# A trunk of attention, retention and convolution on one core: a pool for the operands of the matmuls, longer holds of a PSUM bank, key-value products in column halves, and probabilities scaled by their sum ahead of their transposes

## The chip, the cores and the metric

The kernel runs on one core of a Trainium2 chip. The metric is the device time of the program in microseconds (us). A core has five engines with instruction streams of their own: TensorE (PE in the profile) does matmuls and transposes, and its weight loads are listed apart as PEld; VectorE (DVE) and ScalarE (ACT) do elementwise work, GpSimd (POOL) a few powers, and SyncE (SP) issues the DMAs. Data lie in SBUF, 128 partitions wide; TensorE writes into PSUM, which has 8 banks of 2 KB a partition.

## What is computed

One layer of a causal streaming encoder over 2048 tokens of width 1024, all in float32. On the normalised input one projection feeds three mixers: attention over the own chunk of 64 tokens and 8 chunks before it (6 heads of 64), a gated convolution of 31 taps (256 channels), and retention (6 heads of 64). Their outputs are concatenated and projected, and added to the input. A squared-ReLU MLP of width 4096 follows, and then a gated embedding. Cut to what the change touches:

```python
scores = jnp.einsum('bhncd,bhnkd->bhnck', q, kb).astype(jnp.float32) * (d ** -0.5)
scores = scores + bias[None, :, None]
scores = jnp.where(valid[None, None, :, None, :], scores, -1e30)
probs = jax.nn.softmax(scores, axis=-1).astype(v.dtype)
out = jnp.einsum('bhnck,bhnkd->bhncd', probs, vb)
...
kv = jnp.einsum('bhnmd,bhnme->bhnde', k_dec, vc)
def step(state, kv_c):
    return chunk_decay * state + kv_c, state
...
xf * lax.rsqrt(jnp.mean(xf * xf, axis=-1, keepdims=True) + EPS)
```

## The kernel before

**Tiling.** The tokens are worked in 4 blocks of T = 512 (NB = 4), each block in 4 tiles of 128 (NT = 4). The 6 heads of attention and of retention go in 3 pairs of 128 columns. Activations lie transposed, channels on partitions, in 8 tiles of 128 x 512 (KT = 8).

**Products.** A float32 operand is split into a high part in the matmul's format (fp32r) and the rest, also in fp32r. mm3s then issues three matmuls: high by high, high by low, low by high; it is the three-record group that recurs in the trace. All large products stream 512 or 384 columns. `wunit` brings weights in 1 MB units of HALF = 512 columns into the tile w (6 buffers). In block 0 they come as raw float32 and are split on ScalarE and VectorE (L126, L127); the split form is kept in DRAM, and the later blocks load it whole.

**Where the operands lie.** `big(name, slot)` is a tile of 8 x 512 in one of four buffers big0 to big3 (16 KB a partition each). xh and xl, the split normalised input, use big0 and big1, for the mixers and again (from wo_b, L688, on) for the MLP. mh and ml, the split mixer outputs, use big2 and big3; then hid, the MLP's hidden tile, takes big2 and big3 in turn. `late()` puts the gate's input xh and xl in big2 and big3 for blocks 0 to 2; for the last block ffn2 puts it in big0 and big1. In the matmuls xh, xl, hid, mh and ml are moving operands of 512 columns with blocks of w as weights, but for att_proj and ret_proj, where blocks of xh and xl are the weights and w moves. All of this comes from the pool `sp`, opened after the pool of constants. In the built program w starts at byte 23584 of a partition, big0 and big1 at 72736 and 89120, big2 and big3 at 195712 and 212096.

**Order of the work.** The large products are a chain of segments: per block conv_proj, from block 1 on the gate of the block before, then att_proj and ret_proj for three pairs, wo_a and wo_b (output projection), and eight pairs of ffn1 and ffn2. Each yields after every matmul, and `advance()` then asks whether some other work is due and puts it there: `tasks` at fixed places, and three chains: att_mix (0), ret_mix (1), conv_mix (2). A step of a chain is issued, then its `yield d` sets a hold: the chain's next step comes when `clk`, the planner's own estimate of TensorE's time, is d later. Chains 1 and 2 use one PSUM bank "r" in turn; `rfree` holds either back for 2.0 after the other's step. W lists the holds. TensorE keeps the order so written; the other engines' instructions are ordered by a scheduler from priorities that follow program order, and `tc.high_priority(offset=...)` moves a piece forward or, where negative, back.

**The places that the change touches.**
- rms_split (L230 on) makes xh, xl of the MLP's input, and then the squares and their running sum sq for the norm. norm2 takes the sum when ffn1 has begun.
- att_mix, per token tile t: scores into two banks sc (one a head); a custom VectorE instruction adds the bias and finds the negative maximum nm (L501); ScalarE takes Exp and the row sum into rs (L503); five transposes per head (L59, sc<-ident,pt) and a copy pT; then 20 records of values, po<-pT,v, one tile later. Both the wait for the scores, W["st"], and that for the transposes, W["ts"], are holds. Behind the last tile:

```python
        V.reciprocal(rs[:, 8:16], rs[:, 0:8])
        rb = tmp("rb", T).rearrange("p (t n) -> p t n", n=P)
        V.tensor_copy(rb.rearrange("p t (h d) -> p (t h) d", d=HD),
                      rs[:, 8:16].unsqueeze(2).to_broadcast([P, 8, HD]))
        yield W["vo"]
        ...
            PE.transpose(b[:, i * P : i * P + P], rb[:, i], ident)
        rT = tmp("rT", T)
        A.activation(rT, b[:, :T], AF.Copy)
        values(NT - 1, pT, *span)
        yield 0
        ...
        V.tensor_tensor(rT, po, rT, ALU.mult)
```

- ret_mix: rkv (keys by values, four 128x128 products of which only the two diagonal 64x64 blocks are read by the state updates, L613), then transposes rqT and rkT, scores rsc, their masking rat on VectorE (L638), rout, and a group norm.
- conv_mix: transposes cvt, layer norm z (L402), transposes back cvb, and the pointwise product cpw.

Of the kernel before, what the change touches and what calls it, by code (L numbers as in the profile page):

```python
# [12 lines left out]
F32R = mybir.dt.float32r  # L13
# [20 lines left out]
AHEAD = 2500  # L34
LATE = -1000
AT, RT = (2, 4, 6), (3, 5, 7)
WOA = [(j, k) for ks in ((0, 1, 2, 3), (4, 5)) for j in range(2) for k in ks] + [(j, k) for j in range(2, KT) for k in range(6)]
# [3 lines left out]
def trunk(ctx, tc, a, out):  # L41
# [4 lines left out]
    class PE:  # L46
# [10 lines left out]
        def transpose(o, x, i):  # L57
            clk[0] += 240 / 2200.0
            tc.keep_in_program_order(nc.tensor.transpose(o, x, i))  # L59

    cpool = ctx.enter_context(tc.tile_pool(name="const", bufs=1))
    sp = ctx.enter_context(tc.tile_pool(name="sp", bufs=1))
# [10 lines left out]
    def stile(tag, bufs, shape, name=None, dt=F32):  # L73
        return sp.tile(list(shape), dt, tag=tag, name=name or tag, bufs=bufs)
# [4 lines left out]
    def big(name, slot):  # L79
        return stile(f"big{slot}", 1, [P, 8, T], name, F32R)  # L80

# [40 lines left out]
    def wtile():  # L122
        return stile("w", 6, [P, 2, 2, HALF], "w", F32R)

# [105 lines left out]
    def rms_split(j, gidx, x, sq):  # L230
        h = cur["h"][j]
        g = ng[:, gidx, j : j + 1]
        A.activation(x[0][:, j], h, AF.Copy, scale=g)  # L233
        V.scalar_tensor_tensor(x[1][:, j], h, g, f(x[0][:, j]), ALU.mult, ALU.subtract)  # L234
        if j == 0:
            A.activation(sq, h, AF.Square)
        else:
            q = tmp("q", T)
            A.activation(q, h, AF.Square)
            V.tensor_tensor(sq, sq, q, ALU.add)  # L240

# [18 lines left out]
    cur = {}  # L260
    W = dict(qk=5.0, st=4.5, ts=2.0, vo=1.6, r0=3.5, r1=2.4, r2=1.8, r3=11, c1=5.0, c2=4.0, c3=0.6)

# [120 lines left out]
    def conv_mix():  # L383
# [3 lines left out]
        for u in range(2):  # L387
# [13 lines left out]
            for i in range(2):  # L401
                V.tensor_scalar(z[u][:, i * DC : i * DC + DC], b2[:, i], s6[:, 12 + 2 * i : 13 + 2 * i],  # L402
                                s6[:, 18 + i : 19 + i], ALU.subtract, ALU.mult)
            yield W["c1"]
        hl = []
        for c in range(2):
            b = rbank("cvb")
            for t in range(NT):
                PE.transpose(b[:, t * P : t * P + P], z[t // 2][:, (t % 2) * DC + c * P : (t % 2) * DC + c * P + P], ident)
            u = tmp("u", T)  # L410
            A.activation(ys[c], b, AF.Tanh, bias=cvh[:, 1, c : c + 1], scale=cvh[:, 0, c : c + 1])
            A.activation(u, b, AF.Identity, bias=cvh[:, 1, c : c + 1], scale=cvh[:, 0, c : c + 1])
            V.scalar_tensor_tensor(ys[c], ys[c], 1.0, u, ALU.add, ALU.mult)
            yh, yl = cv("yh", F32R), cv("yl", F32R)
            A.activation(yh, ys[c], AF.Copy)
            V.tensor_tensor(yl, ys[c], f(yh), ALU.subtract)
            hl.append((yh, yl))
            yield W["c2"]
        yield W["c3"]
# [41 lines left out]
    def att_mix(p):  # L461
# [21 lines left out]
        def scores(t):  # L483
# [14 lines left out]
            for h, s in enumerate(ss):  # L498
# [4 lines left out]
                A.activation(pt[:, :n], pt[:, :n], AF.Exp, bias=nm[:, 0:1], scale=-1.0,  # L503
                             accum_out=rs[:, 2 * t + h : 2 * t + h + 1])
                out.append((s, pt, c0 // P, n // P))
            return out
# [29 lines left out]
        for t in range(NT):  # L536
# [6 lines left out]
            if t < NT - 1:  # L543
                rdy = both(t + 1)
        V.reciprocal(rs[:, 8:16], rs[:, 0:8])
        rb = tmp("rb", T).rearrange("p (t n) -> p t n", n=P)
        V.tensor_copy(rb.rearrange("p t (h d) -> p (t h) d", d=HD),
                      rs[:, 8:16].unsqueeze(2).to_broadcast([P, 8, HD]))
        yield W["vo"]
        b = sb2("rT")  # L550
        for i in range(NT):
            PE.transpose(b[:, i * P : i * P + P], rb[:, i], ident)
        rT = tmp("rT", T)
        A.activation(rT, b[:, :T], AF.Copy)
        values(NT - 1, pT, *span)
        yield 0
        kvc[p] = k, v
        mh, ml = mix()
        V.tensor_tensor(rT, po, rT, ALU.mult)
        A.activation(mh[:, AT[p]], rT, AF.Copy)  # L560
        V.tensor_tensor(ml[:, AT[p]], rT, f(mh[:, AT[p]]), ALU.subtract)
        yield 0
# [37 lines left out]
    def ret_mix(p):  # L600
# [7 lines left out]
        for t in range(NT):  # L608
            PE.matmul(b[:, t * P : t * P + P], ns[t][:, P : 2 * P], ns[t][:, 256:384], start=True, stop=True)
        states = [now] + stm + [nxt]  # L610
        for t in range(NT):
            for hr in hrs:
                V.scalar_tensor_tensor(states[t + 1][hr, hr], states[t][hr, hr], gstate[hr, p : p + 1],  # L613
                                       b[hr, t * P + hr.start : t * P + hr.stop], ALU.mult, ALU.add)
        yield W["r0"]
        b = rbank("rqT")
# [5 lines left out]
        A.activation(qT, b, AF.Copy)  # L622
        yield W["r1"]
        b = rbank("rkT")
# [3 lines left out]
        A.activation(kT, b, AF.Copy)  # L628
        yield W["r1"]
        at = stile("rat", 1, [P, NT, 2 * P])  # L630
# [222 lines left out]
    chains = [[], [], []]  # L853
    rfree = [0.0]

    def chain(i, gen, start, end):
# [26 lines left out]
    def advance(pos):  # L883
        posn[0] = pos
        for t in list(tasks):
            while t[0] and t[0][0] <= pos:
# [8 lines left out]
        for c in chains:  # L895
            while c and c[0][0] <= pos:
# [5 lines left out]
                try:  # L902
                    d = next(t[3])
                    t[4] = clk[0] + d + 0.01
                    if c is not chains[0]:
                        rfree[0] = clk[0] + 2.0
                except StopIteration:
# [148 lines left out]
```

## Time and profile before

| | before |
|---|---|
| median of 3 runs | 2718.81 us (2717.66 to 2721.08) |
| the profiled execution's own time | 2718.58 us |
| its span | 2716.6 us |
| granted TensorE clock, mean | 0.996 |
| matmul records on TensorE | 13354 |
| DMA | 533.36 MB, 196 GB/s over the span |

The span is the time from the first to the last instruction that the profile shows; 2.0 us lie around it. Busy time is given per engine. A matmul's record shows how long it is in the array, and successive ones overlap: the pace of a stream is read from the distance of their starts. The granted clock is TensorE's share of its full 2.4 GHz.

### The profile page before, as it was taken

Reading aid. Unit: us, or ns where it says so; the run is one execution under the profiler, and the core shown is the slowest. Engines: PE = TensorE matmul, PEld = TensorE weight load, DVE = VectorE, ACT = ScalarE, POOL = GpSimd, SP = SyncE. Lnnn points to the kernel's source line nnn. Section 1 sums busy time; section 2 is a strip of 40 time slices with the busy share of each in tenths; the row PEclk is TensorE's granted clock in tenths of the full one; section 3 lists DMA queues with packets and bytes.
Section 4 is the critical chain, followed back from the end, with each engine's and each line's share of the span. In section 5 each row is a group of like instructions: output and inputs, shape, how many; then the busy total and the mean of one; then the engine's idle time right before and its main releaser. Section 6 shows DMA issues by size and latency. Waiting matters only on the chain.

```text
span 2716.6 us, 33597 instructions
## 1 busy us (share of the span) xinstructions
PE 2680.4 (99%) x13354; PEld 2216.5 (82%) x13354; DVE 1327.8 (49%) x2649; ACT 764.2 (28%) x1576; POOL 97.0 (4%) x98
## 2 busy tenths in 40 slices
PE   8989999999999999999999999999999999999999
PEld 7777788888888888888888888888888888888887
DVE  7966544458655443334755552222384545222233
ACT  4444423343244222123214331101222432110111
POOL 1010000000010000000001000000000100000000
PEclk9999999999999999999999999999999999999999
DMA  8667656467633567677543455555654354555553
GB/s 285 211 213 244 219 177 208 166 198 267 217 121 140 206 216 261 216 255 261 217 168 121 159 203 192 193 186 191 240 194 170 112 199 142 189 191 187 192 201 125
DMA packets 123708, 533.36 MB, mean 196 GB/s; under 512 B 12832, under 2 KB 39712, under 8 KB 77728
## 3 DMA queue, kind: packets, MB, share of 16 engines
q1 hardware_dynamic: 123552, 531.21, 55.7%
q8 instruction: 106, 1.74, 0.3%
q14 instruction: 50, 0.41, 0.0%
HBM read 410.58 MB, written 120.59 MB: 196 GB/s over the span
## 4 chain that ended last, share of the span: by engine, by line
PE 89%; DVE 6%; DMA 2%; POOL 1%; ACT 1%; issue 1%; SPq 0%; POOLq 0%; DVEq 0%; ACTq 0%
PE acc L54 52%; PE w L54 27%; PE ple L54 2%; PE po L54 2%; PE sc L54 2%; PE sc L59 1%; POOL ass L199 1%; PE rout L54 1%; DVE y L359 1%; PE cvp L54 1%; DMA w<-k_wr 1%; DVE w L127 1%; PE rsc L54 1%; POOL g L199 0%; PE cpw L54 0%
## 5 line engine op out<-in xcount | busy, mean ns | idle before, releaser
L54 PE MATMUL acc<-xh,w 128*128 128x512 f32 (+1 forms) x1744 | 546.7, 389 | 0.0
L54 PE MATMUL acc<-w,xh 128*128 128x512 f32 (+1 forms) x1536 | 457.5, 373 | 1.1 <-DMA w<-k_wr 1.1
L54 PEld LDWEIGHTS acc<-xh,w 128*128 128x128 f32 x1744 | 326.3, 188 | 70.5 <-ACT xh L233 0.2
L54 PE MATMUL acc<-hid,w 128*128 128x512 f32 x1536 | 373.7, 396 | 0.0
L54 PE MATMUL w<-hid,w 128*128 128x512 f32 x1536 | 368.8, 395 | 0.0
L54 PEld LDWEIGHTS w<-hid,w 128*128 128x128 f32 x1536 | 288.5, 188 | 69.9
L54 PEld LDWEIGHTS acc<-hid,w 128*128 128x128 f32 x1536 | 288.7, 188 | 69.7
L54 PE MATMUL acc<-xl,w 128*128 128x512 f32 (+1 forms) x872 | 337.4, 391 | 1.9 <-DVE xl L234 1.9
L54 PE MATMUL w<-xh,w 128*128 128x512 f32 x1024 | 323.3, 391 | 0.0
L54 PEld LDWEIGHTS acc<-w,xh 128*128 128x128 f32 x1536 | 280.8, 189 | 38.9 <-issue 6.3
L126 ACT ACTIVATE w<-raw 128x512 fp32r<-128x512 f32 (+1 forms) x288 | 163.4, 615 | 460.6 <-PE acc L54 190.3
L54 PE MATMUL acc<-w,xl 128*128 128x384 f32 (+1 forms) x768 | 284.2, 370 | 0.0
L721 ACT ACTIVATE hid<-r 128x512 fp32r<-128x512 f32 x128 | 80.0, 625 | 569.3 <-DVE r L720 569.3
L54 PEld LDWEIGHTS w<-xh,w 128*128 128x128 f32 x1024 | 192.8, 189 | 39.7
L54 PE MATMUL w<-xl,w 128*128 128x512 f32 x512 | 200.1, 391 | 0.0
L54 PEld LDWEIGHTS acc<-xl,w 128*128 128x128 f32 x872 | 163.9, 188 | 38.3 <-DVE xl L234 4.2
L127 DVE TENSOR_TENSOR w<-raw,w 128x512 fp32r<-128x512 f32 (+1 forms) x288 | 182.7, 676 | 23.8 <-ACT w L126 23.1
L747 DVE TENSOR_TENSOR h<-h,w 128x512 f32<-128x512 f32 x128 | 88.0, 687 | 205.7 <-PE w L54 205.3
L359 DVE SCALAR_TENSOR_TENSOR y<-gl,cw,y 128x512 f32<-128x512 f32 x240 | 172.5, 745 | 1.9
L747 DVE TENSOR_TENSOR h<-h,acc 128x512 f32<-128x512 f32 x128 | 87.9, 687 | 169.9 <-PE acc L54 169.5
L54 PEld LDWEIGHTS acc<-w,xl 128*128 128x128 f32 x768 | 145.5, 189 | 15.7 <-issue 0.5
L720 DVE SCALAR_TENSOR_TENSOR r<-acc,r 128x512 f32<-128x512 f32 x64 | 44.3, 691 | 210.6 <-PE acc L54 197.7
(177 smaller groups left out, 2811.9 us busy)
## 6 DMA issues: line engine op xcount, KB each, us to landing
w<-k_w SPq DMA_DIRECT2D x160, 1024.0 KB, 4.8
k_w<-w SPq DMA_DIRECT2D x64, 1024.0 KB, 7.1
raw<-in_w_dram SPq DMA_DIRECT2D x96, 512.0 KB, 4.4
w<-k_wr SPq DMA_DIRECT2D x36, 1024.0 KB, 7.1
w<-k_w_g SPq DMA_DIRECT2D x30, 1024.0 KB, 4.8
w<-k_wa SPq DMA_DIRECT2D x36, 768.0 KB, 5.6
w<-k_w_oa SPq DMA_DIRECT2D x18, 1024.0 KB, 7.0
k_wr<-w SPq DMA_DIRECT2D x12, 1024.0 KB, 7.3
```

The costliest lines, as they stand in the source:

```text
L54: tc.keep_in_program_order(nc.tensor.matmul(o, x, y, start=start, stop=stop))
L59: tc.keep_in_program_order(nc.tensor.transpose(o, x, i))
L126: A.activation(w[:, 0, :n], x, AF.Copy)
L127: eng.tensor_tensor(w[:, 1, :n], x, f(w[:, 0, :n]), ALU.subtract)
L199: G.tensor_tensor(o, var, nhalf[:, :n], ALU.pow)
L359: V.scalar_tensor_tensor(y, gl[:, j : j + T], cw[:, c, j : j + 1], y, ALU.mult, ALU.add)
L720: V.scalar_tensor_tensor(r, b, 0.0, cur["r2"], ALU.max, ALU.mult)
L721: A.activation(hid[:, j], r, AF.Square)
L747: V.tensor_tensor(h[j], h[j], b, ALU.add)
```

## The change

- A pool `gp`, opened ahead of the constants, holds the tiles w (6 buffers) and big0 to big3. In the built program w starts at byte 1152 and the four big tiles at 50304, 66688, 83072 and 99456; the constants and all else follow them.
- The squares and sums in rms_split get the offset SQ = -150, behind their place in program order.
- W["st"] is 5.2 for 4.5. A step may yield a pair (d, r), where r replaces the 2.0 for which bank "r" is held: 5.0 and 3.0 in conv_mix, 3.5, 2.4 and 2.4 in ret_mix. In block 0 up to wo_a all these holds are multiplied by 1.2.
- In att_mix each score tile is scaled by the reciprocal of its row sum right after Exp. The reciprocals at the end, their broadcast copy, the rT transposes and copy, and the product of po with rT go; mh and ml are made from po.
- rkv's four 128x128 products become eight of 64x64, only the diagonal blocks.

```diff
@@ -33,6 +33,7 @@
 HALF = 512
 AHEAD = 2500
 LATE = -1000
+SQ = -150
 AT, RT = (2, 4, 6), (3, 5, 7)
 WOA = [(j, k) for ks in ((0, 1, 2, 3), (4, 5)) for j in range(2) for k in ks] + [(j, k) for j in range(2, KT) for k in range(6)]
 
@@ -58,6 +59,7 @@
             clk[0] += 240 / 2200.0
             tc.keep_in_program_order(nc.tensor.transpose(o, x, i))
 
+    gp = ctx.enter_context(tc.tile_pool(name="gp", bufs=1))
     cpool = ctx.enter_context(tc.tile_pool(name="const", bufs=1))
     sp = ctx.enter_context(tc.tile_pool(name="sp", bufs=1))
     dram = ctx.enter_context(tc.tile_pool(name="dram", bufs=1, space=bass.MemoryType.DRAM))
@@ -77,7 +79,7 @@
         return stile("raw", 2, [P, UNIT], name)
 
     def big(name, slot):
-        return stile(f"big{slot}", 1, [P, 8, T], name, F32R)
+        return gp.tile([P, 8, T], F32R, tag=f"big{slot}", name=name, bufs=1)
 
     def anat(name):
         return stile("anat", 5, [P, 256], name)
@@ -120,7 +122,7 @@
 
 
     def wtile():
-        return stile("w", 6, [P, 2, 2, HALF], "w", F32R)
+        return gp.tile([P, 2, 2, HALF], F32R, tag="w", name="w", bufs=6)
 
     def wsplit(w, x, n, eng):
         A.activation(w[:, 0, :n], x, AF.Copy)
@@ -232,12 +234,13 @@
         g = ng[:, gidx, j : j + 1]
         A.activation(x[0][:, j], h, AF.Copy, scale=g)
         V.scalar_tensor_tensor(x[1][:, j], h, g, f(x[0][:, j]), ALU.mult, ALU.subtract)
-        if j == 0:
-            A.activation(sq, h, AF.Square)
-        else:
-            q = tmp("q", T)
-            A.activation(q, h, AF.Square)
-            V.tensor_tensor(sq, sq, q, ALU.add)
+        with tc.high_priority(offset=SQ):
+            if j == 0:
+                A.activation(sq, h, AF.Square)
+            else:
+                q = tmp("q", T)
+                A.activation(q, h, AF.Square)
+                V.tensor_tensor(sq, sq, q, ALU.add)
 
     def rms_rstd(r):
         b = rbank("ms")
@@ -258,7 +261,7 @@
         A.activation(r, b[:, :T], AF.Copy)
 
     cur = {}
-    W = dict(qk=5.0, st=4.5, ts=2.0, vo=1.6, r0=3.5, r1=2.4, r2=1.8, r3=11, c1=5.0, c2=4.0, c3=0.6)
+    W = dict(qk=5.0, st=5.2, ts=2.0, vo=1.6, r0=3.5, r1=2.4, r2=1.8, r3=11, c1=5.0, c2=4.0, c3=0.6)
 
     def xnorm(blk):
         xh, xl = big("xh", 0), big("xl", 1)
@@ -401,7 +404,7 @@
             for i in range(2):
                 V.tensor_scalar(z[u][:, i * DC : i * DC + DC], b2[:, i], s6[:, 12 + 2 * i : 13 + 2 * i],
                                 s6[:, 18 + i : 19 + i], ALU.subtract, ALU.mult)
-            yield W["c1"]
+            yield W["c1"], 5.0
         hl = []
         for c in range(2):
             b = rbank("cvb")
@@ -415,7 +418,7 @@
             A.activation(yh, ys[c], AF.Copy)
             V.tensor_tensor(yl, ys[c], f(yh), ALU.subtract)
             hl.append((yh, yl))
-            yield W["c2"]
+            yield W["c2"], 3.0
         yield W["c3"]
         for c in range(2):
             b = rbank("cpw")
@@ -502,6 +505,9 @@
                                        ALU.add, ALU.min, nm[:, 0:1])
                 A.activation(pt[:, :n], pt[:, :n], AF.Exp, bias=nm[:, 0:1], scale=-1.0,
                              accum_out=rs[:, 2 * t + h : 2 * t + h + 1])
+                ri = rs[:, 8 + 2 * t + h : 9 + 2 * t + h]
+                V.reciprocal(ri, rs[:, 2 * t + h : 2 * t + h + 1])
+                V.tensor_scalar(pt[:, :n], pt[:, :n], ri, None, ALU.mult)
                 out.append((s, pt, c0 // P, n // P))
             return out
 
@@ -542,23 +548,13 @@
             yield W["ts"]
             if t < NT - 1:
                 rdy = both(t + 1)
-        V.reciprocal(rs[:, 8:16], rs[:, 0:8])
-        rb = tmp("rb", T).rearrange("p (t n) -> p t n", n=P)
-        V.tensor_copy(rb.rearrange("p t (h d) -> p (t h) d", d=HD),
-                      rs[:, 8:16].unsqueeze(2).to_broadcast([P, 8, HD]))
         yield W["vo"]
-        b = sb2("rT")
-        for i in range(NT):
-            PE.transpose(b[:, i * P : i * P + P], rb[:, i], ident)
-        rT = tmp("rT", T)
-        A.activation(rT, b[:, :T], AF.Copy)
         values(NT - 1, pT, *span)
         yield 0
         kvc[p] = k, v
         mh, ml = mix()
-        V.tensor_tensor(rT, po, rT, ALU.mult)
-        A.activation(mh[:, AT[p]], rT, AF.Copy)
-        V.tensor_tensor(ml[:, AT[p]], rT, f(mh[:, AT[p]]), ALU.subtract)
+        A.activation(mh[:, AT[p]], po, AF.Copy)
+        V.tensor_tensor(ml[:, AT[p]], po, f(mh[:, AT[p]]), ALU.subtract)
         yield 0
 
     def ret_proj(blk, p):
@@ -606,13 +602,15 @@
         st[p].reverse()
         b = rbank("rkv")
         for t in range(NT):
-            PE.matmul(b[:, t * P : t * P + P], ns[t][:, P : 2 * P], ns[t][:, 256:384], start=True, stop=True)
+            for h, hr in enumerate(hrs):
+                PE.matmul(b[hr, t * P + h * HD : t * P + h * HD + HD], ns[t][:, P + h * HD : P + h * HD + HD],
+                          ns[t][:, 256 + h * HD : 256 + h * HD + HD], start=True, stop=True)
         states = [now] + stm + [nxt]
         for t in range(NT):
             for hr in hrs:
                 V.scalar_tensor_tensor(states[t + 1][hr, hr], states[t][hr, hr], gstate[hr, p : p + 1],
                                        b[hr, t * P + hr.start : t * P + hr.stop], ALU.mult, ALU.add)
-        yield W["r0"]
+        yield W["r0"], 3.5
         b = rbank("rqT")
         for t in range(NT):
             PE.transpose(b[:, t * P : t * P + P], ns[t][:, :P], ident)
@@ -620,13 +618,13 @@
         for h, hr in enumerate(hrs):
             V.tensor_copy(qz[hr, :, h], b[hr].rearrange("p (t n) -> p t n", n=P))
         A.activation(qT, b, AF.Copy)
-        yield W["r1"]
+        yield W["r1"], 2.4
         b = rbank("rkT")
         for t in range(NT):
             PE.transpose(b[:, t * P : t * P + P], ns[t][:, P : 2 * P], ident)
         kT = stile("ro", 1, [P, T], "rk")
         A.activation(kT, b, AF.Copy)
-        yield W["r1"]
+        yield W["r1"], 2.4
         at = stile("rat", 1, [P, NT, 2 * P])
         mask = rm.rearrange("p h n -> p (h n)").unsqueeze(1).to_broadcast([P, 2, 2 * P])
         for u in range(2):
@@ -852,6 +850,7 @@
 
     chains = [[], [], []]
     rfree = [0.0]
+    slow = [1.0]
 
     def chain(i, gen, start, end):
         chains[i].append([start, end, gen, None, 0.0])
@@ -882,6 +881,7 @@
 
     def advance(pos):
         posn[0] = pos
+        slow[0] = 1.2 if pos < at(("woa", 0), 0.0) else 1.0
         for t in list(tasks):
             while t[0] and t[0][0] <= pos:
                 t[0].pop(0)
@@ -901,9 +901,10 @@
                     t[3] = t[2]()
                 try:
                     d = next(t[3])
-                    t[4] = clk[0] + d + 0.01
+                    d, r = d if isinstance(d, tuple) else (d, 2.0)
+                    t[4] = clk[0] + d * slow[0] + 0.01
                     if c is not chains[0]:
-                        rfree[0] = clk[0] + 2.0
+                        rfree[0] = clk[0] + r * slow[0]
                 except StopIteration:
                     c.pop(0)
 
```

Order of VectorE at the end of block 0's wo_b, where the MLP's xl and the squares sq are made. L127 and L129 are splits of raw weights. Before:

```order
L127 TENSOR_TENSOR w<-raw,w 128x512 x2
L234 SCALAR_TENSOR_TENSOR xl<-h,ng,xh 128x512
L240 TENSOR_TENSOR sq<-sq,q 128x512
L234 SCALAR_TENSOR_TENSOR xl<-h,ng,xh 128x512
L240 TENSOR_TENSOR sq<-sq,q 128x512
L234 SCALAR_TENSOR_TENSOR xl<-h,ng,xh 128x512
L240 TENSOR_TENSOR sq<-sq,q 128x512
L234 SCALAR_TENSOR_TENSOR xl<-h,ng,xh 128x512
L240 TENSOR_TENSOR sq<-sq,q 128x512
L234 SCALAR_TENSOR_TENSOR xl<-h,ng,xh 128x512
L240 TENSOR_TENSOR sq<-sq,q 128x512
```

After the change (h<-h,acc adds a product to the residual):

```order
L699 TENSOR_TENSOR h<-h,acc 128x512
L129 TENSOR_TENSOR w<-raw,w 128x512 x2
L236 SCALAR_TENSOR_TENSOR xl<-h,ng,xh 128x512 x4
L243 TENSOR_TENSOR sq<-sq,q 128x512 x2
L129 TENSOR_TENSOR w<-raw,w 128x512 x2
L243 TENSOR_TENSOR sq<-sq,q 128x512 x4
L251 TENSOR_SCALAR rms<-ms 128x4
```

The squares stood between the xl's; now four xl's stand together, and the squares are behind them.

Order of TensorE in block 1 at the end of the first attention pair, where the first projection is att_proj (acc<-w,xh with 384 columns) and ret_proj begins (512 columns). Before:

```order
L54 MATMUL rsc<-qz,rk 128x256 x2
L54 MATMUL acc<-w,xh 128x384
L59 MATMUL rT<-ident,rb 128x128 x4
L54 MATMUL po<-pT,v 64x128 x10
L54 MATMUL acc<-w,xl 128x384
L54 MATMUL acc<-w,xh 128x512
L54 MATMUL rout<-st_189,rq 128x128
```

After:

```order
L55 MATMUL acc<-w,xh 128x384 x2
L55 MATMUL acc<-w,xl 128x384
L55 MATMUL acc<-w,xh 128x512 x2
L55 MATMUL acc<-w,xl 128x512
L55 MATMUL acc<-w,xh 128x512 x2
L55 MATMUL acc<-w,xl 128x512
L55 MATMUL po<-pT,v 64x128 x10
L60 MATMUL cvt<-ident,y 128x128 x4
L55 MATMUL acc<-w,xh 128x512 x2
```

The rT transposes are gone; po, which stood behind them and ahead of the next ret_proj, stands now some rows of it later, with conv_mix's first transposes cvt behind it.

Order of VectorE at about the same place of block 1; ISA pt,nm is the custom instruction that reads the scores, rat the masking of the retention's scores, ass and an the norm of the queries and keys. Before:

```order
L446 TENSOR_REDUCE ass<-sq 128x4
L447 TENSOR_SCALAR ass<-ass 128x4
L449 TENSOR_TENSOR an<-qk,ass 128x256
L516 COPY pT<-sc 128x640
L547 COPY rb<-rs 128x512
L638 TENSOR_TENSOR rat<-rsc,rm 128x512 x2
L559 TENSOR_TENSOR rT<-po,rT 128x512
L446 TENSOR_REDUCE ass<-sq 128x4
L447 TENSOR_SCALAR ass<-ass 128x4
L561 TENSOR_TENSOR ml<-rT,mh 128x512
L449 TENSOR_TENSOR an<-qk,ass 128x256
```

After:

```order
L522 COPY pT<-sc 128x640
L504 ISA pt,nm<-sc,bias 128x640
L504 ISA nm 128x1
L504 ISA pt,nm<-sc,bias 128x640
L504 ISA nm 128x1
L636 TENSOR_TENSOR rat<-rsc,rm 128x512
L509 RECIPROCAL rs<-rs 128x1
L510 TENSOR_SCALAR pt<-pt,rs 128x640
L509 RECIPROCAL rs<-rs 128x1
L510 TENSOR_SCALAR pt<-pt,rs 128x640
L449 TENSOR_REDUCE ass<-sq 128x4
L450 TENSOR_SCALAR ass<-ass 128x4
```

The copy rb and the product rT are gone; behind each pair of score reductions stand two reciprocals and two scalings of pt, and one rat stands ahead of them where two stood together.

## Rows read from the trace of the kernel before

**Rows 1.** The page: busy time by engine, and the chain that ended last.
```profile
PE 2680.4 (99%) x13354; PEld 2216.5 (82%) x13354; DVE 1327.8 (49%) x2649; ACT 764.2 (28%) x1576; POOL 97.0 (4%) x98
...
PE 89%; DVE 6%; DMA 2%; POOL 1%; ACT 1%; issue 1%; SPq 0%; POOLq 0%; DVEq 0%; ACTq 0%
```
**Rows 2.** Windows (us): busy PE, PEld, DVE, ACT, POOL; clock; DMA share; GB/s.
```profile
60.00:100.00 40.00, 36.14 (x189) 29.62 (x187) 37.15 (x89) 17.23 (x52) 1.01 (x1) 0.91 0.73 261
60.00:300.00 240.00, 223.05 (x1200) 182.35 (x1199) 178.19 (x442) 109.18 (x261) 17.14 (x14) 0.96 0.66 231
300.00:2716.00 2416.00, 2405.41 (x11915) 1989.35 (x11913) 1108.74 (x2128) 623.31 (x1254) 70.03 (x61) 1.00 0.54 191
```
**Rows 3.** TensorE's waits: waited for; us in total, times, longest us.
```profile
PE cvb L59 <- DVE z L402: 4.0, 3, 1.3
PE rsc L54 <- DVE rat L638: 3.6, 5, 1.1
PE rkv L54 <- DVE z L402: 3.0, 1, 3.0
PE sc L54 <- DVE pT L516: 2.4, 2, 2.2
...
PE acc L54 <- DVE xl L234: 1.9, 3, 0.8
```
**Rows 4.** Timeline of TensorE, block 1's MLP: start us, us, engine, line, op.
```profile
982.46 0.39 PE L54 MATMUL w<-xh,w 128*128 128x512 f32 x1
...
993.34 0.39 PE L54 MATMUL acc<-xh,w 128*128 128x512 f32 x1
...
998.78 2.98 PE L54 MATMUL acc<-hid,w 128*128 128x512 f32 x12
...
1021.19 0.40 PE L54 MATMUL acc<-xh,w 128*128 128x512 f32 x1
```
**Rows 5.** Timeline of TensorE in the gates of block 0 and block 3.
```profile
678.51 0.39 PE L54 MATMUL ple<-ph,w 128*128 128x512 f32 x1
...
692.47 0.39 PE L54 MATMUL ple<-ph,w 128*128 128x512 f32 x1
...
2676.27 0.40 PE L54 MATMUL ple<-ph,w 128*128 128x512 f32 x1
...
2690.03 0.40 PE L54 MATMUL ple<-ph,w 128*128 128x512 f32 x1
```
**Rows 6.** Timeline of TensorE in block 1: rkv, rT and what follows each.
```profile
768.48 1.05 PE L54 MATMUL rkv<-rn 128*128 128x128 f32 x8
769.28 0.42 PE L54 MATMUL acc<-w,xh 128*128 128x384 f32 x1
...
790.12 0.60 PE L59 MATMUL rT<-ident,rb 128*128 128x128 f32 x4
790.65 1.31 PE L54 MATMUL po<-pT,v 128*64 128x128 f32 x20
```
**Rows 7.** Timeline of block 1: an Exp's sum, and TensorE's next values and transposes.
```profile
759.80 0.19 ACT L503 ACTIVATION_READ_ACCUMULATOR pt<-pt,nm 128x1 f32 x1
...
762.02 1.31 PE L54 MATMUL po<-pT,v 128*64 128x128 f32 x20
763.26 1.31 PE L59 MATMUL sc<-ident,pt 128*128 128x128 f32 x10
```
**Rows 8.** VectorE by line: count | busy us, mean ns of one | idle before, releaser.
```profile
L547 DVE COPY rb<-rs 128x512 f32<-128x512 f32 x12 | 5.0, 418 | 0.0
L357 DVE TENSOR_SCALAR y<-gl,cw,cvec 128x512 f32<-128x512 f32 x8 | 4.3, 541 | 0.0
L545 DVE RECIPROCAL rs<-rs 128x8 f32<-128x8 f32 x12 | 2.4, 202 | 9.9 <-ACT pt L503 9.9
```
**Rows 9.** Timeline at the start of block 0's ffn1: VectorE and TensorE.
```profile
282.48 0.68 DVE L240 TENSOR_TENSOR sq<-sq,q 128x512 f32<-128x512 f32 x1
...
283.87 0.55 PE L54 MATMUL acc<-xl,w 128*128 128x512 f32 x1 [0.77 <-DVE xl L234]
```

## The prediction

> **What bounds the kernel now.** I read the busy line and the chain that ended last first: TensorE is busy for 2680.4 of 2716.6 us and holds 89% of the chain [rows 1]. So only three things can move the time much: the pace of TensorE's matmuls, the instructions it executes, and its idle stretches. The windows place the idle time: from 60 to 300 us, block 0's mixers, TensorE is busy 223.05 of 240 us at a granted clock of 0.96; from 300 us to the end 2405.41 of 2416 at 1.00 [rows 2]. That is 16.9 and 10.6 us of idle time. A mean of 0.96 over 240 us is about 19 us at 1.2 GHz in place of 2.4 GHz, so about 9 us of lost work. The waits name the causes [rows 3]: cvb for z, rsc for the masked scores, rkv for z and the shared bank, sc for a pT copy, and the first ffn1 products that move xl. In the first 40 of those 240 us VectorE is busy 37.15 us [rows 2], so it is VectorE that is late in block 0. Last I looked at the starts of successive matmuls in a clean stretch of the MLP, and this gave the largest term.
>
> **The pool.** The same 128x512 product runs at two paces. The ffn1 products, whose moving operand is xh or xl, go from 982.46 to 993.34 us in 48 matmuls: 226.7 ns each. The ffn2 products right behind, whose moving operand is hid, go from 998.78 to 1021.19 us in 96: 233.4 ns [rows 4]. Weights, shapes, banks and clock are alike; nothing waits. What differs is where the moving tile lies. The gate is a check on this, since its code is the same in every block, but late() puts xh and xl into big2 and big3, and for the last block ffn2 leaves them in big0 and big1: two columns of it take 13.96 us in block 0 (678.51 to 692.47) and 13.76 us at the end (2676.27 to 2690.03) [rows 5]. In the built program of before w starts at byte 23584 of a partition, big0 and big1 at 72736 and 89120, big2 and big3 at 195712 and 212096. The fast places are the low ones, and the ones that share w's offset within 2048 bytes; I can't tell which of the two counts. In the changed program w starts at 1152 and the four big tiles at 50304, 66688, 83072 and 99456: all low, all with w's offset. So both readings say that hid, mh, ml and the early gates now run at the fast pace.
>
> The price: hid is moved by 4 blocks x 8 groups x 32 x 3 = 3072 matmuls, x 6.7 ns = 20.6 us; mh and ml, in the same two buffers, by 4 x 64 x 3 = 768, 5.1 us; 24 early gate columns save 0.10 us each, 2.4 us. Together 28 us. The gate saves only 4 ns on each of its 24 xh and xl products, since the six of ple between them, from buffers that stay high, are slow in both; by that figure hid and mh/ml would give 16 us, 18 with the gate. The long hid streams are nearer to the first row: I take -25. From the other side, were the new place a slow one, everything that is fast today would fall to 233.4 ns: ffn1's 3072, conv's 384, ret_proj's 1152 and the last gate's 192, 4800 x 6.7 = +32 us.
>
> A rule of the Trainium skill speaks against this term. "SBUF — State Buffer", section "Who interferes with whom", gives TensorE one read port for the moving operand and one for the weights, and says that TensorE never waits on anyone; a tile's place would then be free, and this term zero. The trace does not bear that out for the two buffers, 226.7 against 233.4 ns, though the cause could be something other than the place.
>
> **The transposes of the reciprocals.** Four rT transposes leave TensorE's order 12 times: 790.12 to 790.65 us, 0.53 us each time [rows 6], 6.4 us. They hid nothing, as TensorE's stream is dense there: -6.
>
> **The split rkv.** Four 128x128 products (eight records) take from 768.48 to 769.28 us, 0.80 us or 0.10 us a record [rows 6]. Half as many columns in twice as many matmuls: if a record's time goes with its columns, half is saved, 12 x 0.4 = 5 us; if it is a floor, 12 x 0.8 = 10 us is added. The nearest row is po, with 64 output columns: 20 records from 762.02 to 763.26 us, 62 ns each [rows 7]; 16 of those are 1.0 us, +0.2 us each time, and with half po's moving columns less. I take -1.
>
> The Trainium skill's "TensorEngine Tiling (Array Packing)", section "Key Properties", says that a change of tiling mode, not merely of tile, drains TensorE. po and the full-width transposes behind it follow each other here without a gap that I can separate from po's own pace. If such a drain costs what a matmul's 0.39 us exceed its 0.227 us of pace, 0.16 us, then two in each of 12 places are an estimated 4 us, and the sum would be 4 us higher.
>
> **The normalisation.** Each of the 96 score tiles gets a reciprocal and a 128x640 scaling on VectorE, between Exp and the transposes. No such row exists: the reciprocal is bounded by 128x8's 0.20 us; the scaling by the 128x512 COPY's 0.42 us from below and, stretched to 640 columns, the 0.54 us of TENSOR_SCALAR from above, 0.68 [rows 8]. So 0.6 to 0.9 us a tile, 58 to 85 us in all; 12 reciprocals and copies of 0.20 and 0.42 us [rows 8], 7 us, and as many products with rT and ScalarE's rT copies go; mh and ml read po's bank themselves, which takes a step out of their way. VectorE is busy 1108.74 of 2416 us past block 0 [rows 2], so this costs nothing there if each step has time. In block 1 the second Exp is read out at 759.99 us, and TensorE reaches its transposes at 763.26 [rows 7]: 3.3 us of cover against 0.9 us behind the second tile, and st, raised from 4.5 to 5.2, adds 0.7. The order shows what queues behind: two score reductions, two scalings and rat share VectorE, and rsc waits for rat. In block 0 VectorE has no room: 12 steps x 1.8 us, of which I let 5 us reach TensorE. Without any cover it would be 48 x 1.8 = 86 us.
>
> **The holds and the squares.** A hold is time in the planner's estimate; a longer one puts more projection matmuls before the next use of the bank. c1's 5.0 for 2.0, times 1.2 in block 0, covers rkv's 3.0 us and the three 1.3 us waits of cvb for z. The retention's 3.5 and 2.4 add 0.4 to 2.2 us, about the size of rsc's longest, 1.1. The score reads' holds grow by 1.2 alone, so sc's 2.2 us wait for pT may stay. Squares at lower priority leave the xl's together: in before a square of 0.68 us stands between two xl's, and TensorE waits 0.77 us [rows 9]; in the new order four xl's follow each other. What is late next is the row of norm2: two weight splits and four squares stand ahead of it on VectorE, 2 x 0.68 + 4 x 0.68 = 4.1 us at a square's 0.68, and norm2 starts 0.4 of 32 x 3 products later, 38 x 227 ns = 8.7 us, so that stays hidden. Of block 0's 16.9 us I count 10 as gone and 5 given back by the normalisation: -5. With half of the stalls about half of the 9 us of lost clock returns: -4. Past block 0, cvb's 4.0 and most of rsc's share go: of 10.6 us idle, -4. No projection matmul is added by a hold; they only change places. Were none of this to come, 0; were all, 16.9 + 10.6 + 9, -36.
>
> **Sum.** From the profiled run's own 2718.6 us (span 2716.6 and 2.0 around it; the median shown is 2718.8): -25 -6 -1 -5 -4 -4 = -45, so 2673 us.
>
> **The rivals.**
> (B) The buffers' place is not the cause, or the new one is no better: everything but the pool term comes, 2718.6 - 20 = 2699 us. For it: nothing in the trace varies the place alone. Against it: the gate, whose code is the same. The rule of the Trainium skill named above ("SBUF — State Buffer", "Who interferes with whom") would give this case.
> (C) The fast pace belongs to today's place of big0, big1 and w, and not to what I read from it: hid stays slow and the 4800 fast matmuls join it, +32 - 20 = +12, 2731 us. It is slower than before from the point where about 3800 of them fall, 25 us. Against it: two different addresses are fast today, 16 KB apart, with all six weight slots.
> (D) The normalisation takes the stalls' place: VectorE in block 0 is later by two scalings in every step, transposes wait 12 x 1.8 us = 22 us, and the clock stays down, so nothing of the 13 us comes and some 10 more go: -25 -6 -1 +10 = 2697 us. For it: VectorE's 37.15 of 40 us. It would be slower than before only if the later blocks' 36 steps waited over 0.8 us each too; their 3.3 us of cover speaks against that.
> (E) The change doesn't do what it says: the holds are in estimated time, and a bank's reader may be as late as before: -25 -6 -1 = 2687 us.
>
> **Chances.** Forecast 0.63, E 0.10, D 0.11, B 0.11, C 0.05. The range reaches from 2655 (all stalls and clock go) to 2708, past B, D and E. About 0.2%, 5.4 us, is what a measurement of this kernel can tell from no change. The forecast, B, D and E are all faster than that, with a little of B and D lost to "same" or beyond: 0.88 faster, 0.05 same, 0.07 slower, which is C and the far end of D.
>
> **What would show it.** In the new profile acc<-hid should step by 226 to 228 ns like acc<-xh, and two gate columns in block 0 by about 13.8 us. If hid stays at 233, B holds; if xh rises to 233, C. rT must be gone, and rkv must take between 0.5 and 1.8 us. The waits should lose rkv for z, cvb for z and acc for xl; a new wait of sc (the transposes) for the scaled pt, above all from 60 to 300 us, would be D, and the granted clock there tells the rest. The forecast fails if TensorE's idle time from 60 to 300 us doesn't fall below about 13 us, or if hid doesn't speed up.

## The result, and the profile after

The changed kernel takes 2687.52 us (median of 4 runs, 2685.50 to 2689.66), the kernel before 2718.23 beside it: a ratio of 0.9886, with a 95% interval of 0.9869 to 0.9903. The profiled execution took 2686.37 us, its span 2684.6: 32.2 us less than the profiled run before, where 45 were forecast.

Of the page after, the lines of [rows 1] (busy time by engine; the chain):

```profile
PE 2644.8 (99%) x13402; PEld 2206.5 (82%) x13402; DVE 1372.8 (51%) x2805; ACT 757.6 (28%) x1564; POOL 95.9 (4%) x98
...
PE 92%; DVE 4%; DMA 2%; ACT 1%; POOL 1%; issue 0%; SPq 0%; DVEq 0%; ACTq 0%; POOLq 0%
```

TensorE's busy time fell by 36 us, more than the span; so its idle time grew by 4. Its timeline in block 1's MLP, answering to [rows 4]:

```profile
972.73 0.39 PE L55 MATMUL w<-xh,w 128*128 128x512 f32 x1
...
983.38 0.39 PE L55 MATMUL w<-xh,w 128*128 128x512 f32 x1
...
989.05 2.88 PE L55 MATMUL acc<-hid,w 128*128 128x512 f32 x12
...
1010.81 0.39 PE L55 MATMUL acc<-xh,w 128*128 128x512 f32 x1
```

The 96 matmuls of hid now take 989.05 to 1010.81 us, 226.7 ns each for 233.4; xh and xl are as before (47 starts, 10.65 us, 226.6 ns). In the early gate, answering to [rows 5], two columns take 13.74 us for 13.96:

```profile
669.74 0.40 PE L55 MATMUL ple<-ph,w 128*128 128x512 f32 x1
...
671.14 0.39 PE L55 MATMUL acc<-xh,w 128*128 128x512 f32 x1
...
683.48 0.40 PE L55 MATMUL ple<-ph,w 128*128 128x512 f32 x1
```

rkv, answering to [rows 6], takes 0.61 us for 0.80. But the matmul ahead of it now takes 0.27 us to rkv's start (758.28 to 758.55), where the one before took 0.18 (768.30 to 768.48); first the changed kernel, then the line of the kernel before that stands ahead of rkv:

```profile
758.28 0.34 PE L55 MATMUL acc<-w,xh 128*128 128x384 f32 x1
758.55 0.69 PE L55 MATMUL rkv<-rn 128*64 128x64 f32 x16
759.16 0.44 PE L55 MATMUL acc<-w,xh 128*128 128x384 f32 x1
```

```profile
768.30 0.34 PE L54 MATMUL acc<-w,xh 128*128 128x384 f32 x1
```

The windows, answering to [rows 2] (span and busy times of PE, PEld, DVE, ACT, POOL; clock; DMA share; GB/s), show what did not come. From 60 to 300 us TensorE idles 18.4 us where it idled 16.9, at the same 0.96, and from 300 us to the end 12.4 for 10.6:

```profile
60.00:100.00 40.00, 35.69 (x189) 29.79 (x187) 37.69 (x100) 17.41 (x52) 2.02 (x2) 0.91 0.74 261
60.00:300.00 240.00, 221.63 (x1232) 182.51 (x1231) 186.59 (x484) 108.34 (x260) 16.39 (x14) 0.96 0.66 234
300.00:2684.00 2384.00, 2371.56 (x11934) 1979.61 (x11932) 1145.83 (x2243) 618.14 (x1244) 69.61 (x61) 1.00 0.54 193
```

TensorE's waits, answering to [rows 3] (us in total, times, longest), are other ones. Those of cvb for z, rsc for rat, rkv for z, sc for pT and acc for xl are all gone; in their places:

```profile
PE cvt L60 <- DVE y L362: 7.6, 1, 7.6
...
PE cvt L60 <- DVE z L405: 6.7, 3, 2.2
PE rkT L60 <- ACT rq L620: 5.3, 2, 2.7
PE ms L55 <- DVE sq L243: 2.3, 2, 1.7
PE cpw L55 <- DVE ml L431: 1.6, 1, 1.6
```

The longest stands at 151.65 us, in block 0. conv_mix's first transposes cvt are reached at 143.80 us and wait for y, the last of the 60 steps of the depthwise convolution on VectorE; before and between its last two steps stand two reciprocals and two scalings of pt (timeline, VectorE and TensorE):

```profile
149.38 0.37 DVE L509 RECIPROCAL rs<-rs 128x1 f32<-128x1 f32 x2
149.67 0.73 DVE L362 SCALAR_TENSOR_TENSOR y<-gl,cw,y 128x512 f32<-128x512 f32 x1
150.32 0.61 DVE L510 TENSOR_SCALAR pt<-pt,rs 128x256 f32<-128x256 f32 x2
150.85 0.75 DVE L362 SCALAR_TENSOR_TENSOR y<-gl,cw,y 128x512 f32<-128x512 f32 x1
...
151.65 0.69 PE L60 MATMUL cvt<-ident,y 128*128 128x128 f32 x2 [7.58 <-DVE y L362]
```

In the kernel before, the last step of y began at 143.16 us and cvt, at 146.17, waited for nothing:

```profile
143.16 0.75 DVE L359 SCALAR_TENSOR_TENSOR y<-gl,cw,y 128x512 f32<-128x512 f32 x1
...
146.17 0.60 PE L59 MATMUL cvt<-ident,y 128*128 128x128 f32 x4
```

The normalisation's four instructions shown above are only some 0.8 us of this wait. In the changed kernel three steps of y were still to come at 144 us; they came out between weight splits, the retention's rotation and score reductions, which take most of the time up to 151.65 us. Which part of the change left them there is a question for the experiments. VectorE's rows for the added work (count | busy us, mean ns | idle before): 63.8 us in 192 instructions, near the lower end of the 58 to 85 forecast.

```profile
L510 DVE TENSOR_SCALAR pt<-pt,rs 128x640 f32<-128x640 f32 (+4 forms) x96 | 48.5, 510 | 2.5
...
L509 DVE RECIPROCAL rs<-rs 128x1 f32<-128x1 f32 x96 | 15.3, 160 | 10.3 <-ACT pt L506 8.8
```

### The profile page after: what moved, and what is told of

The parts are those of the page before. It is cut to its first block, busy times and chain, and to the rows that moved or that the text cites. A ratio compares the mean times of both kernels' runs of the same rounds, so it can differ in the third digit from the quotient of the medians.

```text
span 2684.6 us, 33820 instructions
## 1 busy us (share of the span) xinstructions
PE 2644.8 (99%) x13402; PEld 2206.5 (82%) x13402; DVE 1372.8 (51%) x2805; ACT 757.6 (28%) x1564; POOL 95.9 (4%) x98
## 4 chain that ended last, share of the span: by engine, by line
PE 92%; DVE 4%; DMA 2%; ACT 1%; POOL 1%; issue 0%; SPq 0%; DVEq 0%; ACTq 0%; POOLq 0%
PE acc L55 53%; PE w L55 27%; PE sc L60 2%; PE po L55 2%; PE sc L55 2%; PE ple L55 2%; PE rout L55 1%; PE cvp L55 1%; DVE w L129 1%; DVE y L362 1%; PE rsc L55 1%; DMA w<-k_wr 1%; POOL ass L201 0%; PE cpw L55 0%; PE qkT L60 0%
## 5 line engine op out<-in xcount | busy, mean ns | idle before, releaser
L55 PE MATMUL acc<-hid,w 128*128 128x512 f32 x1536 | 363.1, 389 | 0.0
L55 PE MATMUL w<-hid,w 128*128 128x512 f32 x1536 | 358.6, 389 | 0.0
L129 DVE TENSOR_TENSOR w<-raw,w 128x512 fp32r<-128x512 f32 (+1 forms) x288 | 182.8, 677 | 21.5 <-ACT w L128 20.9
```

The lines of the kernel that those rows point to most:

```text
L55: tc.keep_in_program_order(nc.tensor.matmul(o, x, y, start=start, stop=stop))
L129: eng.tensor_tensor(w[:, 1, :n], x, f(w[:, 0, :n]), ALU.subtract)
```

## The experiments

Two questions were open: is it the place of the tiles, and which property of it, that sets the pace; and where did the 13 us of stalls and clock go.

**The pool alone (e1) and all but the pool (e2).** e1 is the kernel before with these lines, every engine's order unchanged; e2 is the changed kernel with the reverse.

```diff
+    gp = ctx.enter_context(tc.tile_pool(name="gp", bufs=1))
...
-        return stile(f"big{slot}", 1, [P, 8, T], name, F32R)
+        return gp.tile([P, 8, T], F32R, tag=f"big{slot}", name=name, bufs=1)
...
-        return stile("w", 6, [P, 2, 2, HALF], "w", F32R)
+        return gp.tile([P, 2, 2, HALF], F32R, tag="w", name="w", bufs=6)
```

> The kernel before, with only w and the four big tiles moved into a pool of their own, opened first; every engine's order is that of before. Theory 1, the pool is worth its 28 us of matmul pace and the rest of the change nothing or a loss: about 2691 us (2688 to 2696), hid at 226 to 228 ns a matmul, waits as before. Rival, the pool's place is not the cause of the pace in the changed kernel: within 5 us of before, hid at 233 ns.

> The changed kernel with w and the big tiles back in the old pool, everything else of the change kept. Theory 1: the rest of the change is worth -2 to -6 us, rT's 6 us less some new waits, so 2712 to 2717 us, with hid at 233 ns and the same new waits (cvt for y and z, rkT for rq) as in the changed kernel. Rival, the rest was worth the 20 us forecast and the pool less: 2698 us.

e1: 2690.94 us, ratio 0.9900 (0.9886 to 0.9915), 27.0 us under the 2717.94 of before. e2: 2714.29 us, 0.9988 (0.9979 to 0.9998), 3.7 under it. Together 30.7, which is the change's own 30.7: the parts add up, and everything but the pool is worth 3.7 us. In e2 cvt waits 7.7 us for y, so that wait doesn't come from the pool. In e1's ffn2 of block 1, 24 matmuls of hid take 5.44 us; in e2, from 997.63 us on, 5.60:

```profile
995.77 5.60 PE L54 MATMUL w<-hid,w 128*128 128x512 f32 x24
1001.21 5.60 PE L54 MATMUL acc<-hid,w 128*128 128x512 f32 x24
```

**The place: low with another offset (e3, e12), high with the same (e4).** All three build on e1. e3 puts a pool gq of 24 words, 96 bytes, between w's pool and that of the big tiles, gb; e12 one of 64 words, 256 bytes. e4 opens the big tiles' pool last, at the top of SBUF (163200 to 228735), and moves w to 1408 (a small tile, hist, goes ahead of it), so that both have one offset modulo 2048. Shown is what e3 adds between the pools, and the tile that fills it:

```diff
+    gq = ctx.enter_context(tc.tile_pool(name="gq", bufs=1))
+    gb = ctx.enter_context(tc.tile_pool(name="gb", bufs=1))
...
+        G.memset(gq.tile([P, 24], F32, tag="pad", name="pad"), 0.0)
```

> As the pool alone, but with 96 bytes between w and the big tiles, so that these lie low (50400 to 115935) and 96 bytes off w's offset within 2048 bytes, as big2 and big3 did before. If the offset against the weights sets the pace: hid, xh and xl all step by about 233 ns, and the time is some 30 us over before's, near 2750 us. If it is the low place: 227 ns and about 2691 us.

> As the pool alone, but the big tiles lie at the top of SBUF (163200 to 228735) and w at 1408, all with the same offset within 2048 bytes. If the offset sets the pace: 227 ns and about 2691 us. If it is the low place: 233 ns everywhere and near 2750 us.

> As the pool alone with 256 in place of 96 bytes between w and the big tiles. Each weight block starts a multiple of 512 bytes from w's start and each moving row a multiple of 2048 from its tile's. If the two starts must agree within 512 bytes for the fast pace: 233 ns for hid and xh and about 2744 us, as with 96. If it is enough that they agree within 256 or fewer bytes: 227 ns and about 2691 us.

e3: 2743.85 us; e4: 2687.80; e12: 2689.90 (one run each, before 2717.9 beside e3 and e4 and 2720.9 beside e12). TensorE's timeline in block 1's MLP, e3 first, then e4, then e12:

```profile
990.43 0.40 PE L54 MATMUL w<-xh,w 128*128 128x512 f32 x1
...
1001.63 0.40 PE L54 MATMUL acc<-xh,w 128*128 128x512 f32 x1
...
1010.03 5.76 PE L54 MATMUL w<-hid,w 128*128 128x512 f32 x24
1015.63 5.76 PE L54 MATMUL acc<-hid,w 128*128 128x512 f32 x24
```

```profile
990.60 5.60 PE L54 MATMUL w<-hid,w 128*128 128x512 f32 x24
996.04 5.60 PE L54 MATMUL acc<-hid,w 128*128 128x512 f32 x24
```

```profile
993.72 5.60 PE L54 MATMUL w<-hid,w 128*128 128x512 f32 x24
999.16 5.60 PE L54 MATMUL acc<-hid,w 128*128 128x512 f32 x24
```

Twenty-four matmuls take 5.60 us at e3's offset of 96 bytes, 233.3 ns each, low as the tiles are, and 5.44 us, 226.7 ns, at the top of SBUF with w's offset. xh and xl, fast in the kernel before, are slow in e3: 48 matmuls from 990.43 to 1001.63 us, 233.3 ns each. So it isn't the low place; it is where the moving tile starts against the weights. Nor is it the moving tile's own alignment: big2 of the kernel before, at 195712, and big0 of the changed one, at 50304, both start 1152 bytes past a multiple of 2048, and the first was slow, the second is fast.

With 256 bytes between them the pace is the fast one too: the starts need not agree modulo 512, but at most modulo 256. The gate's products hold two more distances. In the built program of before ph and pl start at 172640 and then every 2048 bytes, 64 bytes past w's offset modulo 512, and six of their products take 1.38 us, 230 ns each; in that of the changed kernel they start at 205408, 480 bytes past it, and six take 1.40 us (669.74 to 671.14 above), 233 ns. So 64 bytes doesn't give the fast pace either, though one nearer to it than 96 does. The line that ends the six in the kernel before, whose first is the 678.51 of [rows 5]:

```profile
679.89 0.39 PE L54 MATMUL acc<-xh,w 128*128 128x512 f32 x1
```

What is left is agreement modulo 128 or modulo 256; 128 bytes was not tried, and why the distance counts no run here shows.

**The rest: normalisation and holds, each undone and both (e5 to e7), and the squares (e8).** e5 is the changed kernel with the normalisation of before, e6 with st=4.5, bank r held 2.0 and factor 1.0, e7 with both, e8 with SQ = 0.

```diff
 e5
-                V.reciprocal(ri, rs[:, 2 * t + h : 2 * t + h + 1])
-                V.tensor_scalar(pt[:, :n], pt[:, :n], ri, None, ALU.mult)
...
+        V.tensor_tensor(rT, po, rT, ALU.mult)
...
 e6
...
-        slow[0] = 1.2 if pos < at(("woa", 0), 0.0) else 1.0
+        slow[0] = 1.0 if pos < at(("woa", 0), 0.0) else 1.0
...
-                    d, r = d if isinstance(d, tuple) else (d, 2.0)
+                    d, r = d[0] if isinstance(d, tuple) else d, 2.0
 e8
-SQ = -150
+SQ = 0
```

> The changed kernel, but with the normalisation of before (one reciprocal, broadcast copy, rT transposes, product of po with rT at the end of each pair); pool, holds, squares and split rkv as in the changed kernel. Theory N, the scalings of pt load VectorE and make y late in block 0: without them cvt's 7.6 us wait for y goes and the clock there with it, the 6.4 us of rT come back, so 2684 to 2689 us, no different from the changed kernel. Rival H, the holds alone cause the new waits: cvt's wait for y stays and rT is added, 2693 to 2695 us.

> The changed kernel with the holds of before (st 4.5, bank r held 2.0, factor 1.0 in block 0); normalisation ahead of the transposes, pool, squares and split rkv as in the changed kernel. Theory H, the longer holds only exchange waits (cvt for z 6.7 and rkT for rq 5.3 in place of cvb for z 4.0 and rsc for rat 3.6): 2684 to 2690 us, with the old waits back. Rival, they hide what they were forecast to hide, and the normalisation costs that much: 2695 us or more.

> The changed kernel with both the normalisation and the holds of before: what stays of the change is the pool, the squares' priority and the split rkv. Pool -27.0 (measured alone), rkv 12 x 0.19 = -2.3, squares about 0: 2686 to 2690 us if these add up. If normalisation and holds help only together: 2688 or so here while each alone is over 2692.

> The changed kernel with the squares at their old priority; TensorE's order is the same. If the offset trades one wait for another: ms for sq (2.3 us) goes, acc for xl (1.9 us) comes back, and the time is within 3 us of the changed kernel's 2687.5. If the squares' priority is worth its xl waits: 2690 us or more with ms unchanged.

| | holds of before | new holds |
|---|---|---|
| normalisation of before | e7: 2686.28 us, 0.9884 (0.9868 to 0.9901) | e5: 2679.14 us, 0.9856 (0.9842 to 0.9871) |
| new normalisation | e6: 2688.74 us, 0.9894 (0.9879 to 0.9908) | changed kernel: 2687.52 us, 0.9886 (0.9869 to 0.9903) |

Neither theory named what e5 shows. The holds are worth 7.1 us beside the old normalisation and 1.2 beside the new one, where the two kernels' times overlap; the new normalisation costs 8.4 us by the medians with the new holds (7.2 when each kernel is counted from the runs of before beside it), and 2.5 with the old. e7, which has neither, is as fast as the changed kernel (0.9884 and 0.9886): normalisation and holds together are worth nothing. e5 is faster than both kernels, with four rT transposes back in each of 12 places. Its window from 60 to 300 us and its longest waits past the start:

```profile
60.00:300.00 240.00, 229.04 (x1275) 188.31 (x1275) 183.73 (x451) 113.08 (x270) 17.72 (x14) 0.98 0.66 236
```

```profile
PE cvt L60 <- DVE z L405: 5.4, 3, 1.8
PE rkT L60 <- ACT rq L627: 3.7, 2, 2.2
PE cpw L55 <- DVE ml L431: 1.7, 1, 1.7
PE ms L55 <- DVE sq L243: 1.7, 1, 1.7
```

TensorE idles 11.0 us there, against 18.4 with the new normalisation and 16.9 before, and the clock is 0.98: this is what the holds were forecast to do, and the wait for y is not there. In e6, with the old holds, cvt waits 4.5 us for y and most of the old waits are back. But in e7 cvt waits 3.1 us for y too, with neither the scalings nor the new holds, and in e5 the last step of y ends at 144.2 us, just as cvt begins. So y is at the edge in all these orders. The scalings cause the wait beside the new holds (7.6 us with them, none without) and little of it beside the old (4.5 and 3.1). e8, 2687.23 us in one run, trades ms for sq (gone) for 1.9 us of acc for xl (back): the squares' priority moves nothing that can be measured.

**Where the normalisation costs, and how (e9, e10), and a step of the convolution (e11).** e9 is the changed kernel that normalises as before in block 0 and ahead of the transposes in blocks 1 to 3. e10 is the changed kernel with block 0's conv_mix begun later. e11 is e9 with a longer step behind each of conv_mix's two cvt in blocks 1 to 3.

```diff
 e9
+                if kprev is not None:
+                    V.reciprocal(ri, rs[:, 2 * t + h : 2 * t + h + 1])
+                    V.tensor_scalar(pt[:, :n], pt[:, :n], ri, None, ALU.mult)
...
 e10
-            chain(2, conv_mix, at(("ap", b, 2), 0.1), at(("rp", b, 2), 0.9))
+            chain(2, conv_mix, at(("ap", b, 2), 0.4), at(("rp", b, 2), 0.9))
 e11 (with e9's lines)
-            yield W["c1"], 5.0
+            yield (W["c1"] if slow[0] > 1 else 7.5), 5.0
```

> The changed kernel, but block 0 normalises as before (rT and the product at the end of each pair), and blocks 1 to 3 ahead of the transposes. If the normalisation's loss lies in block 0, where VectorE is full: from the old normalisation's 2679.1 us nine of the twelve rT groups go, 9 x 0.53 = 4.8 us, so 2672 to 2677 us, without cvt's wait for y. If the scalings cost time in blocks 1 to 3 as well: 2679 us or more.

> The changed kernel, but block 0's convolution mixer starts 0.3 of a projection segment later, which puts its transposes behind the second pair's rkv and retention steps. If the normalisation harms by making y late and nothing else: the 7.6 us wait and some 2 to 3 us of lost clock go, 2677 to 2681 us. If VectorE's load comes out elsewhere, another wait (cvb, cpw, or the first product of wo_a) takes its place: 2684 to 2690 us.

> As the normalisation in blocks 1 to 3 only, and with conv_mix's step from one cvt to the next 7.5 in place of 5.0 in blocks 1 to 3. If cvt's 2.2 us wait for z there is only a step that comes too early: three of them go, 5 to 6 us less than without it, 2667 to 2670 us. If the bank hands the wait on to the next step: no difference, 2672 to 2677 us.

e9: 2677.69 us, 0.9855 (0.9840 to 0.9870), 9.8 us under the changed kernel by the medians: block 0 is where the normalisation costs. In blocks 1 to 3 it gains 1.4 us by the medians against e5, which is no difference by the intervals, where nine rT groups less are 4.8; the number lies just outside what I expected. Of the missing 3 us, cvt's wait for z shows 1.3 (6.7 for 5.4). The granted clock shows the rest: right behind two of these three waits, in blocks 2 and 3, it fell to 1.2 GHz for a while, and it did not in e5. From 1440 to 1460 us it is 0.91, first e9, then e5:

```profile
1440.00:1460.00 20.00, 17.79 (x99) 14.42 (x97) 12.33 (x38) 5.89 (x16) 4.71 (x4) 0.91 0.17 62
```

```profile
1440.00:1460.00 20.00, 18.23 (x115) 14.60 (x114) 14.33 (x52) 7.25 (x20) 4.72 (x4) 1.00 0.19 63
```

From 2105 to 2125 us it is 0.91 and 1.00 again. A clock lower by 0.09 over 20 us, twice, is an estimated 3.6 us of work. The changed kernel has two such falls past block 0 as well, 0.91 from 780 to 800 and from 1450 to 1470 us, where the kernel before has 1.00.

e10: 2687.46 us, 0.9887 (0.9870 to 0.9903), no gain. cvt's wait for y is gone, and sc now waits 3.2 us for pT and cpw 2.2 for u, with the clock at 0.94 from 180 to 300 us. TensorE's idle time from 60 to 300 us fell by 2.2 us, to 16.2. So taking away the wait for y in this way gives nothing. That it is VectorE's load which comes out elsewhere fits this, but is argued and not shown: the later start also leaves conv_mix less room behind it.

e11: 2671.98 us, 0.9833 (0.9819 to 0.9848), the fastest kernel here: 45 us under the 2716.99 of before beside it, and 15.5 under the changed kernel by the medians. cvt's three waits for z, 6.7 us, are gone, with the falls of the clock behind them (1.00 from 1450 to 1470 us), and new waits of sc and cpw are some 4 us; 5.7 us are gained against e9, as expected, though the time is 2 us above the range that I had named.

## Why the prediction was right, and where not

The time lies in the range and the direction is right; 2673 was 14.5 us too low. Measured apart, each from the runs of before beside it, the terms came out as -27.0 for -25 (the pool, e1), -3.8 for -1 (rkv and squares, e7 against e1), -7.1 for -18 (the holds with the clock, ahead of the 5 given back; e5 against e7) and +7.2 for -1 (the normalisation with its 5 and rT's 6; the changed kernel against e5). Two terms made the miss, the holds by 11 us and the normalisation by 8; the other two took 5 of it back. By my own sign, idle time below 13 us from 60 to 300 us, the forecast for block 0 failed: it is 18.4.

- **The pool, -25:** measured alone, -27.0. The mechanism held, and the two readings that I could not tell apart are now told apart: offset against w, not height (e1, e3, e4). Where everything was at the wrong offset (e3) the kernel lost 26 us where the bound said 32.
- **rT, -6:** the records are gone, 6.4 us of TensorE's time by [rows 6], but what replaced them cost more: the 7 to 8 us are what it costs after this gain.
- **rkv, -1:** the size came out, by two parts. A record's time fell from 0.10 to 0.04 us, 12 x 0.19 = -2.3. But rkv's records now have another tiling mode (128*64) than the matmuls around them, and these lose time: in e7 the matmul ahead of rkv takes 0.27 us to the next start and the one behind it 0.38 (1494.14 to 1494.41 and 1495.02 to 1495.40 us), in e1, with the old rkv, 0.17 and 0.35. That leaves some 0.08 us a time, 0.9 us in all. The loss is there, as a drain would make it, but 1.4 us in all and not the 4 of the prediction's estimate. The other 3 us of the -3.8 are open. And my bound of half saved was no bound: half the columns in twice the matmuls are as many columns.
- **The holds, squares and clock, -5 -4 -4:** this step failed. I counted 10 us of block 0's idle time as gone, 4 past it and 4 of clock, and "5 given back by the normalisation". The holds did take the named waits away, but other waits came for them (cvt for z, rkT for rq, 9.1 us in e5), and they gain 7.1 us and not 18 even beside the old normalisation (e5 and e7). And I priced the normalisation and the holds each by itself: with the scalings on VectorE the holds' gain was 1.2 (2.4 counted from the runs of before), and nothing of the clock came back from 60 to 300 us (0.96 before and after).
- **The normalisation, hidden past block 0:** the 3.3 us of cover held; no transposes wait for pt in the changed kernel (with the old holds they wait 1.9 us, e6). But the work it hid behind wasn't idle in block 0: VectorE was busy 37.15 of the first 40 us [rows 2], and what was pushed back was the work of lowest priority, y, on which another mixer's transposes waited.
- **What is late next:** I asked it of the squares and found nothing late; ms did wait 1.7 us for sq in block 0, about the 1.9 that xl had cost.
- **The rivals:** B and C fell with e1. D had the right engine and place, VectorE in block 0, and the wrong waiter: not the transposes of pt but cvt for y. E's sum, 2687, is the measured time, but that is luck: the holds did work, and the normalisation took their gain and rT's.

## What to carry to other kernels

When a matmul stream has no waits left, compare the start-to-start pace of equal products by where their moving operand lies: here 6.7 ns in 227, and 27 us of the kernel, hung on whether tile and weights start at the same offset (0 or 256 bytes apart, modulo 512). Work given to an engine that is "49% busy" costs by the stage where that engine is full; ask which of its low-priority work is pushed back and who waits for that. Two edits that share an engine are to be priced together: the holds gained 7.1 us beside the old normalisation and 1 to 2 beside the new one, so some 5 us went in the pair.

## What was not expected of the hardware

The pace of a 128x512 fp32r matmul depends on the start of the moving tile against that of the weights: 226.7 ns at distances of 0 and 256 bytes, about 230 at 64, 233.3 ns at 96, all modulo 512. Both paces were seen with the moving tile near byte 50000 of the partition (e1 and e3) and near byte 195000 (e4 and the kernel before). Nothing in the waits or the clock shows it.
